# Two-layer recurrence-and-attention trunk on one core: the first probability scalings are pinned behind the second half of q on ScalarE, and their transposes move one chunk on

## The chip, the core and the metric

The kernel runs on one core of one Trainium2 chip. Five engines work side by side on it: TensorE (PE in the rows; its weight loads are PEld), VectorE (DVE), ScalarE (ACT), GpSimd (POOL) and SyncE (SP, which here only starts DMAs). Each engine takes its own instructions strictly in their order and waits on semaphores for the others. The metric is the device time of one execution in microseconds (us).

## The reference

A token batch of 256 x 1024 in float32 runs through two equal layers. Cut to what matters here:

```
for each of 2 layers:
    h  = rms_norm(x)                     # 256 x 1024
    z  = h @ w_in                        # one combined input projection
    A) recurrent half (width 512):
       x = causal_depthwise_conv(z_x, conv_w) + conv_b          # 4 taps
       r, i = sigmoid(x @ w_r), sigmoid(x @ w_i)                # block-diagonal
       h_t = a_t * h_(t-1) + sqrt(1 - a_t^2) * (i * x)_t        # a = exp(-8 r softplus(-lam))
       out_A = h * silu(z_g)
    B) attention half (width 512, 8 query heads of 64, 2 kv heads):
       q, k with rms_norm and partial rotary positions
       compressed branch: blocks of 32 tokens -> two small products -> kc, vc; softmax over blocks
       selected branch:   gathered key blocks, softmax;  window branch: softmax
       out_B = (g0 * o_cmp + g1 * o_sel + g2 * o_win) * silu(z_n)
    x = x + concat(out_A, out_B) @ w_out
```

With 256 tokens, the selected blocks and the window cover all keys that a token may see, and the kernel computes both branches with dense causal attention: softmax probabilities of the scores, each multiplied by its gate over its row sum.

## The kernel before

**Products.** Each large projection is done as three products (`mm3`, L175 to L177) of a high and a low part of both operands. For each 128-column piece of the weights, a "chunk", SP loads it to `raw`, the high part `wh` is a ScalarE cast (L167) or a second DMA by POOL, and VectorE computes the low part `wl` (L170, "the split"). Chunk by chunk, TensorE multiplies 8 pieces of the input by these, 24 products of 128x256 each.

**Chunks.** In each layer some chunks for keys, values, queries and the compressed branch come first. Then come twelve chunks of the recurrent input and of the two gate paths, in the order x0, x1, x2, x3, n0, n1, g0, g1, g2, g3, n2, n3 (numbers 0 to 11), then eight of the output projection (12 to 15 for its first half). The work around a chunk is planned in `plan[n]`, with two lists: one traced ahead of chunk n, one in its middle. The numbers in the table `SL` say where a piece stands: for instance `turn` holds for each of the eight attention pairs (i, t) the chunk ahead of which its probabilities are transposed, i being one of four pairs of query heads and t one of two halves of the tokens; each (i, t) has four score matrices, two heads in two branches. A scheduler then decides the order on each engine from the order of tracing and from dependencies, so a piece can end up a little before or behind its planned place.

**Pieces that the change or the rows touch.**

- `qk_transpose(t)` (t = 0 planned at chunk 0, t = 1 at chunk 2): TensorE transposes keys and queries into PSUM buffers `pp` (there are two). Per kv head ScalarE casts the keys (`kd`, L375 and L376) and VectorE computes their low part (`kl`, L377). Likewise per kv head ("half") the queries, on ScalarE (`qs`, L384) and VectorE (`qs` low part, L385). L387 copies `qT`.
- `att_scores(i, t)`: three products into PSUM (L581, L582, L583), row maxima on VectorE (L586, L588), exponentials on ScalarE into `pr` (L594).
- `att_coef(i, t)`: VectorE makes gate over row sum (L599, L600), ScalarE scales the probabilities by it (L607, four instructions).
- `att_turn(i, t)`: TensorE transposes the scaled probabilities into a `pp` buffer (L620), ScalarE copies them to `pt` (L83).
- The compressed branch: `cmp_act` (L470 `hth` on ScalarE, L472 `hs` on VectorE), `cmp_kv` (L477, L478 products of `hs`, then small steps on VectorE, POOL and ScalarE up to the copy `kcd`, L495), `cmp_kt` (L499, the transpose of `kcd`, and L501), its scores (L511 to L533) and their transposed probabilities `pct`.
- `rg_x(j)`: VectorE writes `xpad` (L652), ScalarE starts the convolution `cx` (L653), VectorE adds three taps (L655). `rg_gates(j)`: L663, two products per j of `cx`, planned at chunks 2 to 5, then activations (L666 on).
- Splits of chunks x2, x3 and n0, n1 are ordered behind `L.qk_done`, the last subtraction of `qk_transpose`.

Of the kernel before, what the change touches and what calls it, by code (L numbers as in the profile page):

```python
# [14 lines left out]
AF = mybir.ActivationFunctionType  # L15
# [9 lines left out]
HD = 64  # L25
# [13 lines left out]
for _n, _w in (("g", 8), ("cw", 16), ("cb", 4), ("br", 4), ("bi", 4), ("lam", 4)):  # L39
# [11 lines left out]

K = dict(scale="A", ev1="A", hid="A", pct="A")
SL = dict(qk=(0, 2), order=("x0", "x1", "x2", "x3", "n0", "n1", "g0", "g1", "g2", "g3", "n2", "n3"),
          cmp=(2, 3, 4), att=(1, 3, 3, 4, 6, 7, 10, 11), turn=(2, 4, 5, 6, 8, 10,
          12, 13), cs=(5, 5), cpt=6, aout=(7, 15), gates=(2, 3, 4, 5), tab=6, sqrt=5,
          scan=8, rout=(9, 11))

# [14 lines left out]
def hybrid_trunk_kernel(ctx: ExitStack, tc: tile.TileContext, vx, wc, wt, wv, wf, wo, w1, w2, pe,  # L72
# [6 lines left out]
    V, A, G, T = nc.vector, nc.scalar, nc.gpsimd, nc.tensor  # L79
# [10 lines left out]
    def bank(tag, bufs, shape=(P, 512), dt=F32):  # L90
        return ps.tile(list(shape), dt, name=tag, tag=tag, bufs=bufs)
# [166 lines left out]
    def layer(l, prev):  # L258

        L = Layer()  # L260
# [105 lines left out]
        def qk_transpose(t):  # L366
            zn = L.zn[t]
            tok = slice(t * P, (t + 1) * P)
            pk = bank("pp", 2)
            for i in range(2):  # L370
                T.transpose(pk[:, i * P:(i + 1) * P],
                            zn[:, 8 + 2 * i:10 + 2 * i].rearrange("p h d -> p (h d)"), ident)
            for g in range(2):
                src = pk[g * HD:(g + 1) * HD, :2 * P].rearrange("p (b s) -> p b s", s=P)
                A.copy(L.kd[:HD, g, :, tok], src)  # L375
                A.copy(L.kd[HD:, g, :, tok], src)  # L376
                V.tensor_tensor(kl[:HD, g, :, tok], src, L.kd[:HD, g, :, tok].bitcast(F32), op=ALU.subtract)  # L377
            pq = bank("pp", 2)
            for i in range(4):
                T.transpose(pq[:, i * P:(i + 1) * P], zn[:, 2 * i:2 * i + 2].rearrange("p h d -> p (h d)"),  # L380
                            ident)
            for g in range(2):
                src = pq[g * HD:(g + 1) * HD].rearrange("p (i s) -> p i s", s=P)
                A.copy(L.qs[:HD, g::2, tok], src)  # L384
                L.qk_done[t] = V.tensor_tensor(L.qs[HD:, g::2, tok], src, L.qs[:HD, g::2, tok].bitcast(F32),  # L385
                                               op=ALU.subtract)
            A.copy(L.qT[:, :, tok], pq.rearrange("p (i s) -> p i s", s=P))  # L387
# [209 lines left out]
        def att_coef(i, t):  # L597
            pr, sm = L.att[i, t]
            V.reciprocal(sm[:, 2], sm[:, 1])  # L599
            V.tensor_tensor(sm[:, 3].rearrange("p (g b) -> p g b", g=2), L.gate[:, t, i, :, 1:3],  # L600
                            sm[:, 2].rearrange("p (g b) -> p g b", g=2), op=ALU.mult)
            for g in range(2):
                for b in range(2):
                    sc_ = sm[:, 3, 2 * g + b:2 * g + b + 1]
                    e = K["scale"][(2 * g + b) % len(K["scale"])]
                    if e == "A":
                        A.activation(pr[g][:, b], pr[g][:, b], AF.Copy, scale=sc_)  # L607
                    else:
                        V.tensor_scalar(pr[g][:, b], pr[g][:, b], sc_, None, op0=ALU.mult)

# [142 lines left out]
        for k in range(KT):  # L753
            b = []
# [22 lines left out]
        def at(n, f, *a, mid=False):  # L777
            plan[n][1 if mid else 0].append(F(f, *a))

        at(1, cmp_hid)  # L780
        at(SL["qk"][0], qk_transpose, 0)
        at(SL["qk"][1], qk_transpose, 1)
        for n, f in zip(SL["cmp"], (cmp_act, cmp_kv, cmp_kt)):
            at(n, f)
        for q in range(8):
            i, t = divmod(q, 2)
            n = SL["att"][q]
            at(n, att_scores, i, t)
            at(n, att_coef, i, t, mid=True)
        at(SL["cs"][0], cmp_scores)  # L790
        at(SL["cpt"], cmp_pt)
        for q in range(8):
# [24 lines left out]
    for l in range(DEPTH):  # L817
        prev, st_ = layer(l, prev)
        prev0 = prev0 or prev
        steps += st_  # L820
# [140 lines left out]
```

## Time and profile before

| | |
|---|---|
| time, median of 3 runs | 250.75 us (250.7 to 250.95) |
| the profiled execution's own time | 250.6 us |
| its span, from first to last instruction | 248.8 us |
| granted TensorE clock, mean of the span | 0.998 |
| TensorE busy | 241.5 us, 97% of the span |
| VectorE, ScalarE, POOL busy | 195.7, 163.9, 40.6 us |

The profile shows one execution. Its span begins with the first instruction of an engine and ends with the last; the device time holds 1.8 us more. A row of a timeline gives the start of an instruction in us from the start of the span, its duration, the engine, the line, the operation, the tile written and the tile read, shapes, a count where neighbours with one form stand together, and in brackets the time that the engine had stood idle before it and what released it. Ends of matmuls are modelled.

### The profile page before, as it was taken

The page shows a single profiled execution, that of the slowest core. Times are in us where ns is not written, and L with a number is a line of the kernel's source. Part 1 is how long each engine was busy: PE and PEld are TensorE (multiplying, and loading weights), DVE is VectorE, ACT ScalarE, POOL GpSimd, SP SyncE. Part 2 cuts the span into 40 slices and gives each one's busy share as a digit, 9 for nine tenths or more (in the row PEclk, how much of TensorE's full clock was granted, in tenths as well). Part 3 has the DMA queues.
Part 4 walks back from the last instruction along what each step waited for, and adds up shares of the span by engine and source line. Part 5 has one row for each costly group of instructions (what it writes and reads, how often), then busy time and mean ns, then how long its engine had stood idle before and what let it go on. Part 6 is the DMA issues. An engine that isn't in the chain of part 4 may idle for free.

```text
span 248.8 us, 5206 instructions
## 1 busy us (share of the span) xinstructions
PE 241.5 (97%) x1958; PEld 222.2 (89%) x1958; DVE 195.7 (79%) x379; ACT 163.9 (66%) x414; POOL 40.6 (16%) x65
## 2 busy tenths in 40 slices
PE   8999999989999999999999999998999999999994
PEld 3999998967998899989999999996889989998993
DVE  5998897789999997555995569688998998875322
ACT  6957429799999968623863553849999996860000
POOL 0027540001901011000001054100100001010000
PEclk9999999999999999999999999999999999999999
DMA  6988999846599778841569968575259848960022
GB/s 216 365 300 261 362 414 402 256 151 192 200 302 401 263 230 277 258 131 52 169 211 354 309 227 263 166 228 188 99 167 335 323 124 262 339 205 19 3 84 84
DMA packets 17593, 57.17 MB, mean 230 GB/s; under 512 B 2208, under 2 KB 3360, under 8 KB 17056
## 3 DMA queue, kind: packets, MB, share of 16 engines
q1 hardware_dynamic: 12816, 39.86, 46.9%
q0 software_dynamic: 4608, 16.78, 21.2%
q8 instruction: 15, 0.25, 0.4%
q10 hardware_dynamic: 144, 0.20, 0.2%
q14 instruction: 10, 0.08, 0.1%
HBM read 55.78 MB, written 1.05 MB: 228 GB/s over the span
## 4 chain that ended last, share of the span: by engine, by line
PE 66%; ACT 14%; DVE 9%; DMA 4%; POOL 3%; issue 2%; SPq 0%; ACTq 0%; DVEq 0%; POOLq 0%
PE fm L175 12%; PE fm L176 12%; PE fm L177 11%; PE pp L620 4%; PE s L175 3%; PE s L177 3%; PE s L176 3%; PE m L634 3%; DVE wl L170 3%; ACT pr L594 3%; DMA ga<-in_gains_dram 2%; ACT qs L384 2%; PE m L637 1%; PE m L640 1%; PE pp L177 1%
## 5 line engine op out<-in xcount | busy, mean ns | idle before, releaser
L170 DVE TENSOR_TENSOR wl<-raw,wh 128x1024 fp32r<-128x1024 f32 (+4 forms) x67 | 74.5, 1118 | 7.4 <-ACT wh L167 3.0
L175 PE MATMUL fm<-hh,wh 128*128 128x256 f32 x192 | 56.9, 296 | 0.1
L176 PE MATMUL fm<-hl,wh 128*128 128x256 f32 x192 | 55.1, 287 | 0.0
L177 PE MATMUL fm<-hh,wl 128*128 128x256 f32 x192 | 54.4, 284 | 0.0
L167 ACT CAST wh<-raw 128x768 fp32r<-128x768 f32 (+4 forms) x34 | 30.5, 896 | 25.4 <-DMA raw<-in_wc_dram 7.0
L175 PEld LDWEIGHTS fm<-hh,wh 128*128 128x128 f32 x192 | 36.7, 191 | 1.4 <-issue 0.8
L176 PEld LDWEIGHTS fm<-hl,wh 128*128 128x128 f32 x192 | 36.8, 191 | 0.5 <-issue 0.4
L177 PEld LDWEIGHTS fm<-hh,wl 128*128 128x128 f32 x192 | 36.7, 191 | 0.0
L594 ACT ACTIVATE pr<-s,sm 128x128 f32<-128x128 f32 (+1 forms) x64 | 25.9, 417 | 7.7 <-DVE sm L588 5.4
L175 PE MATMUL fm<-yy,wh 128*128 128x256 f32 x96 | 27.4, 285 | 0.0
L176 PE MATMUL fm<-yy,wh 128*128 128x256 f32 x96 | 27.0, 281 | 0.0
L177 PE MATMUL fm<-yy,wl 128*128 128x256 f32 x96 | 26.9, 280 | 0.0
L607 ACT ACTIVATE pr<-pr,sm 128x128 f32<-128x128 f32 (+1 forms) x64 | 23.7, 455 | 2.1 <-DVE sm L600 2.0
L175 PEld LDWEIGHTS fm<-yy,wh 128*128 128x128 f32 x96 | 18.1, 188 | 0.8 <-issue 0.8
L156 POOL DMA_DIRECT2D wh<-in_wo_dram x16 | 8.4, 528 | 61.2 <-PE fm L177 26.5
L176 PEld LDWEIGHTS fm<-yy,wh 128*128 128x128 f32 x96 | 18.1, 188 | 0.0
L177 PEld LDWEIGHTS fm<-yy,wl 128*128 128x128 f32 x96 | 18.1, 188 | 0.0
L176 PE MATMUL s<-wl,hh 128*128 128x384 f32 x48 | 16.7, 348 | 0.3 <-DVE wl L170 0.3
L156 POOL DMA_DIRECT2D wh<-in_wf_dram x16 | 9.0, 563 | 47.0 <-PE fm L177 23.4
L177 PE MATMUL s<-wh,hl 128*128 128x384 f32 x48 | 16.1, 336 | 0.0
L620 PE MATMUL pp<-cst,pr 128*128 128x128 f32 x96 | 15.0, 276 | 1.2 <-DVE kl L377 1.2
L729 DVE TENSOR_TENSOR head<-head,fm 128x512 f32<-128x512 f32 x11 | 7.6, 687 | 10.7 <-PE fm L177 10.7
(206 smaller groups left out, 614.9 us busy)
## 6 DMA issues: line engine op xcount, KB each, us to landing
raw<-in_wf_dram SPq DMA_DIRECT2D x24, 512.0 KB, 4.4
wh<-in_wf_dram POOLq DMA_DIRECT2D x16, 512.0 KB, 4.5
raw<-in_wo_dram SPq DMA_DIRECT2D x16, 512.0 KB, 4.8
wh<-in_wo_dram POOLq DMA_DIRECT2D x16, 512.0 KB, 4.8
raw<-in_wt_dram SPq DMA_DIRECT2D x15, 384.0 KB, 4.2
yy<-in_w_dram SPq DMA_DIRECT2D x4, 1024.0 KB, 7.1
raw<-in_wc_dram SPq DMA_DIRECT2D x4, 512.0 KB, 5.3
raw<-in_wv_dram SPq DMA_DIRECT2D x4, 420.0 KB, 4.6
```

Of the source, the lines that this page charges most:

```text
L156: G.dma_start(self.wh, self.src)
L167: A.copy(hi[:, c], self.raw[:, c])
L170: V.tensor_tensor(lo[:, c], self.raw[:, c], hi[:, c].bitcast(F32), op=ALU.subtract)
L175: T.matmul(o, lh, rh, start=start, stop=False)
L176: T.matmul(o, lh, rl, start=False, stop=False)
L177: T.matmul(o, ll, rh, start=False, stop=stop)
L384: A.copy(L.qs[:HD, g::2, tok], src)
L594: A.activation(pr[g][:, b], ov[:, b], AF.Exp, bias=sm[:, 0, 2 * g + b:2 * g + b + 1], accum_out=sm[:, 1, 2 * g + b:2 * g + b + 1])
L607: A.activation(pr[g][:, b], pr[g][:, b], AF.Copy, scale=sc_)
L620: T.transpose(pp[:, (2 * g + b) * P:(2 * g + b + 1) * P], pr[g][:, b, c * P:(c + 1) * P], ident)
L634: T.matmul(o[g * HD:(g + 1) * HD], L.vv[:, 0, b, g * HD:(g + 1) * HD], pt[:, g, b, 0:2].rearrange("p a s -> p (a s)"), start=h == b == 0, ...
L729: V.tensor_tensor(x_sb[:, m], x_sb[:, m], os_[0].rearrange("p (a s) -> p a s", a=2), op=ALU.add)
```

## The change

The last cast of a q half on ScalarE is remembered as `L.qs_done`. The coefficients and scalings of the first pair (0, 0) are no longer planned in the middle of chunk 1 (x1) but ahead of chunk 2 (x2), after `qk_transpose(1)`, and the four scalings are ordered behind the second half of q: no semaphore, only a place in ScalarE's queue. The transposes of that pair are planned at chunk 3 instead of 2. This holds in both layers.

```
-          cmp=(2, 3, 4), att=(1, 3, 3, 4, 6, 7, 10, 11), turn=(2, 4, 5, 6, 8, 10,
+          cmp=(2, 3, 4), att=(1, 3, 3, 4, 6, 7, 10, 11), turn=(3, 4, 5, 6, 8, 10,
           12, 13), cs=(5, 5), cpt=6, aout=(7, 15), gates=(2, 3, 4, 5), tab=6, sqrt=5,
...
             for g in range(2):
                 src = pq[g * HD:(g + 1) * HD].rearrange("p (i s) -> p i s", s=P)
-                A.copy(L.qs[:HD, g::2, tok], src)
+                L.qs_done = A.copy(L.qs[:HD, g::2, tok], src)
...
                     if e == "A":
-                        A.activation(pr[g][:, b], pr[g][:, b], AF.Copy, scale=sc_)
+
+                        with tc.issue_after(L.qs_done.ins) if i == t == 0 else nullcontext():
+                            A.activation(pr[g][:, b], pr[g][:, b], AF.Copy, scale=sc_)
...
             at(n, att_scores, i, t)
-            at(n, att_coef, i, t, mid=True)
+            if q == 0:
+                at(SL["qk"][1], att_coef, i, t)
+            else:
+                at(n, att_coef, i, t, mid=True)
```

Lines behind the pinned scalings have numbers higher by 2 after the change (L607 is L609, L620 is L622, L653 is L655, L663 is L665).

The order of instructions shows what the scheduler makes of it. ScalarE, layer 0, around chunks x1 and x2 before the change (`kd` and `qs` are key and query casts of token half 1, `pr` the probabilities of pair (0, 0), `cx` the convolution):

```order
L376 CAST kd_122<-pp 64x2x128
L607 ACTIVATE pr<-pr,sm 128x128 x4
L653 ACTIVATE cx<-xpad_72,head 128x256
L375 CAST kd_122<-pp 64x2x128
L376 CAST kd_122<-pp 64x2x128
L384 CAST qs<-pp 64x4x128
L470 ACTIVATE hth<-m 128x160
L666 ACTIVATE rr<-fm,hb 128x256
L667 ACTIVATE tmp_747<-fm,hb 128x256
L669 ACTIVATE tl<-rr,sp 128x256
L83 COPY pt<-pp 128x4x128
L384 CAST qs<-pp 64x4x128
```

The same place after the change:

```order
L376 CAST kd_122<-pp 64x2x128
L655 ACTIVATE cx<-xpad_72,head 128x256
L384 CAST qs<-pp 64x4x128
L375 CAST kd_122<-pp 64x2x128
L376 CAST kd_122<-pp 64x2x128
L470 ACTIVATE hth<-m 128x160
L668 ACTIVATE rr<-fm,hb 128x256
L384 CAST qs<-pp 64x4x128
L609 ACTIVATE pr<-pr,sm 128x128 x4
L387 COPY qT<-pp 128x4x128
L669 ACTIVATE tmp_740<-fm,hb 128x256
```

The four scalings moved from ahead of the second key half to behind the second q half, and that q half moved from behind three gate activations and the `pt` copy to behind one gate activation.

TensorE, layer 0, at the end of chunk x2 before the change (`fm` products are those of the chunk, `s` are scores, `m` the compressed branch):

```order
L177 MATMUL fm<-hh,wl 128x256
L620 MATMUL pp<-cst,pr 128x128 x4
L175 MATMUL fm<-hh,wh 128x256
L176 MATMUL fm<-hl,wh 128x256
L177 MATMUL fm<-hh,wl 128x256
L175 MATMUL fm<-hh,wh 128x256
L176 MATMUL fm<-hl,wh 128x256
L177 MATMUL fm<-hh,wl 128x256
L581 MATMUL s<-kd_122,qs 128x512
L477 MATMUL m<-w2s,hs 32x64
L478 MATMUL m<-w2s,hs 128x64
L582 MATMUL s<-kl,qs 128x512
```

After the change the scores that follow the whole of chunk x2 end like this, and chunk x3 begins:

```order
L581 MATMUL s<-kd_122,qs 128x256
L582 MATMUL s<-kl,qs 128x256
L583 LDWEIGHTS identb
L583 MATMUL s<-maskb,identb 128x256
L622 MATMUL pp<-cst,pr 128x128 x4
L665 MATMUL fm<-cx,rws 128x256 x2
L175 MATMUL fm<-hh,wh 128x256
```

The transposes of pair (0, 0) moved from the middle of x2's products to behind the scores, and the scores of pair (1, 0), of 256 columns, moved up from behind x3 to stand here.

VectorE, layer 1, around the weight splits of the first gate chunks, before:

```order
L600 TENSOR_TENSOR sm<-gate,sm 128x4
L501 TENSOR_TENSOR kcb<-m,cst 128x32
L655 SCALAR_TENSOR_TENSOR cx<-xpad_72,head,cx 128x256
L586 TENSOR_REDUCE sm<-s 128x2
L655 SCALAR_TENSOR_TENSOR cx<-xpad_72,head,cx 128x256
L586 TENSOR_REDUCE sm<-s 128x2
L170 TENSOR_TENSOR wl<-raw,wh 128x1024 x2
L599 RECIPROCAL sm<-sm 128x4
```

And after:

```order
L600 TENSOR_TENSOR sm<-gate,sm 128x4
L501 TENSOR_TENSOR kcb<-m,cst 128x32
L586 TENSOR_REDUCE sm<-s 128x2 x2
L170 TENSOR_TENSOR wl<-raw,wh 128x1024
L657 SCALAR_TENSOR_TENSOR cx<-xpad_72,head,cx 128x256
L170 TENSOR_TENSOR wl<-raw,wh 128x1024
L657 SCALAR_TENSOR_TENSOR cx<-xpad_72,head,cx 128x256
L599 RECIPROCAL sm<-sm 128x4
L170 TENSOR_TENSOR wl<-raw,wh 128x1024
L657 SCALAR_TENSOR_TENSOR cx<-xpad_72,head,cx 128x256
```

The three taps of the last `cx` of the layer moved behind and between weight splits; their consumers are the gate products planned at chunk 5.

## Rows read from the trace of the kernel before

**Rows 1.** The page: busy time, share of the span and number of instructions of each engine; the granted clock in 40 slices (tenths); the shares by engine of the chain that ended last.

```profile
PE 241.5 (97%) x1958; PEld 222.2 (89%) x1958; DVE 195.7 (79%) x379; ACT 163.9 (66%) x414; POOL 40.6 (16%) x65
...
PEclk9999999999999999999999999999999999999999
...
PE 66%; ACT 14%; DVE 9%; DMA 4%; POOL 3%; issue 2%; SPq 0%; ACTq 0%; DVEq 0%; POOLq 0%
```

**Rows 2.** Timeline of TensorE, layer 0, end of chunk x2 and start of x3 (at 56.05). Columns: start us, duration us, engine, line, operation, written and read tiles, partitions of weights and products, shape, count, idle time before.

```profile
50.23 0.28 PE L176 MATMUL fm<-hl,wh 128*128 128x256 f32 x1
50.35 0.28 PE L177 MATMUL fm<-hh,wl 128*128 128x256 f32 x1
51.54 0.63 PE L620 MATMUL pp<-cst,pr 128*128 128x128 f32 x4 [0.91 <-DVE kl L377]
...
53.03 0.30 PE L477 MATMUL m<-w2s,hs 128*32 128x64 f32 x2
53.26 0.43 PE L478 MATMUL m<-w2s,hs 128*128 128x64 f32 x2
...
53.95 1.03 PE L663 MATMUL fm<-cx,rws 128*128 128x256 f32 x4
54.63 0.58 PE L581 MATMUL s<-kd,qs 128*128 128x512 f32 x1
...
56.05 0.36 PE L175 MATMUL fm<-hh,wh 128*128 128x256 f32 x1
```

**Rows 3.** Timeline of ScalarE, layer 0, same place: scalings, `cx`, key and query casts, a gate activation.

```profile
48.12 1.28 ACT L607 ACTIVATE pr<-pr,sm 128x128 f32<-128x128 f32 x4
49.31 0.59 ACT L653 ACTIVATE cx<-xpad,head 128x256 f32<-128x256 f32 x1
49.92 0.37 ACT L375 CAST kd<-pp 64x256 fp32r<-64x256 f32 x1
...
50.69 0.58 ACT L384 CAST qs<-pp 64x512 fp32r<-64x512 f32 x1
...
51.37 0.46 ACT L666 ACTIVATE rr<-fm,hb 128x256 f32<-128x256 f32 x1
...
53.17 0.58 ACT L384 CAST qs<-pp 64x512 fp32r<-64x512 f32 x1
```

**Rows 4.** Timeline of VectorE, layer 0: `hs` and the last q subtraction.

```profile
52.53 0.32 DVE L472 SCALAR_TENSOR_TENSOR hs<-hth,m 128x160 f32<-128x160 f32 x1
...
53.79 0.69 DVE L385 TENSOR_TENSOR qs<-pp,qs 64x512 fp32r<-64x512 f32 x1 [0.45 <-ACT qs L384]
```

**Rows 5.** Timeline of TensorE, layer 0, end of chunk x3.

```profile
59.01 0.40 PE L581 MATMUL s<-kd,qs 128*128 128x512 f32 x1
...
59.60 1.03 PE L663 MATMUL fm<-cx,rws 128*128 128x256 f32 x4
60.56 0.24 PE L499 MATMUL m<-cst,kcd 32*128 32x32 f32 x1
...
61.30 0.28 PE L583 MATMUL s<-maskb,identb 128*128 128x256 bf16 x1
61.87 0.39 PE L581 MATMUL s<-kd,qs 128*128 128x256 f32 x1 [0.28 <-ACT pr L594]
```

**Rows 6.** Timeline of TensorE, layer 1: end of x2, then end of x3 (n0 starts at 181.03).

```profile
170.41 0.28 PE L177 MATMUL fm<-hh,wl 128*128 128x256 f32 x1
171.50 0.30 PE L477 MATMUL m<-w2s,hs 128*32 128x64 f32 x2 [0.80 <-DVE hs L472]
...
172.04 0.63 PE L620 MATMUL pp<-cst,pr 128*128 128x128 f32 x4 [0.25 <-DVE kl L377]
...
179.57 0.60 PE L663 MATMUL fm<-cx,rws 128*128 128x256 f32 x2
180.10 0.24 PE L499 MATMUL m<-cst,kcd 32*128 32x32 f32 x1
...
181.03 0.39 PE L175 MATMUL fm<-hh,wh 128*128 128x256 f32 x1
```

**Rows 7.** Timeline of VectorE: the copy of `kcd` in layer 0 and in layer 1.

```profile
59.98 0.20 DVE L495 COPY kcd<-kcd 32x64 f32<-32x64 f32 x1
...
179.62 0.18 DVE L495 COPY kcd<-kcd 32x64 f32<-32x64 f32 x1
```

**Rows 8.** Timeline of VectorE, layer 1: `hs`.

```profile
171.12 0.32 DVE L472 SCALAR_TENSOR_TENSOR hs<-hth,m 128x160 f32<-128x160 f32 x1
```

**Rows 9.** Timeline of ScalarE, layer 1: eight scalings, of pairs (0, 1) and (1, 0).

```profile
181.62 2.88 ACT L607 ACTIVATE pr<-pr,sm 128x256 f32<-128x256 f32 x8
```

**Rows 10.** What leads to the gate products of chunk 5. Timelines of VectorE and TensorE, layer 1, then layer 0: the last taps of `cx`, a row maximum, two weight splits, the gate products.

```profile
184.12 0.69 DVE L586 TENSOR_REDUCE sm<-s 128x2 f32<-128x512 f32 x1
184.72 2.35 DVE L170 TENSOR_TENSOR wl<-raw,wh 128x1024 fp32r<-128x1024 f32 x2
...
188.31 1.02 PE L663 MATMUL fm<-cx,rws 128*128 128x256 f32 x4
...
69.20 0.47 DVE L655 SCALAR_TENSOR_TENSOR cx<-xpad,head,cx 128x256 f32<-128x256 f32 x1
...
69.88 1.03 PE L663 MATMUL fm<-cx,rws 128*128 128x256 f32 x4
```

**Rows 11.** Timeline of VectorE, layer 1: a weight split that waited for its transfer.

```profile
190.56 1.23 DVE L170 TENSOR_TENSOR wl<-raw,wh 128x1024 fp32r<-128x1024 f32 x1 [0.54 <-DMA raw<-in_wf_dram]
```

## The prediction, made before the changed kernel ran

> **What bounds the kernel now.** I read the page first, then the chain of work that ended last, then the timelines of TensorE, ScalarE and VectorE around the first attention scores of each layer. On the page the reader is to see that TensorE is busy 97% of the span at the full granted clock (2.4 GHz), that it carries 66% of the chain, and that ScalarE and VectorE together carry 23% of it [rows 1]. So time can only be won where TensorE stands still because one of those two is late. Its timeline is read by starts: within a chunk one 128x256 product starts 0.12 us after the other [rows 2], so a longer distance is a hole. Four holes lie where the change works, two in each layer.
>
> Layer 0, end of chunk x2: the product at 50.35 is followed by the transposes of the first probabilities only at 51.54, so 1.07 us are lost [rows 2]. They wait for a PSUM buffer `pp` that the second key half (kl) still has to leave; kl is late because the four scalings (48.12 to 49.31) stand ahead of the second half's casts on ScalarE [rows 3]. Layer 0, end of x3: a score product of (2,0) waits from 61.42 to 61.87, 0.45 us [rows 5]. Layer 1, end of x2: hs, the compressed-key input, holds L477 from 170.53 to 171.50, 0.97 us, and the transposes follow 0.54 us later where 0.23 us is usual (53.03 to 53.26), 0.31 us more [rows 2, 6].
>
> How long a hole is depends on the reading. The idle column gives 0.91, 0.28, 0.80 and 0.25 us, 2.24 together [rows 2, 5, 6]; starts give 1.07, 0.45, 0.97 and 0.31, 2.80. I take starts, since the idle column counts from a modelled end of a product, 0.28 us after its start, while the next may begin after 0.12. The Trainium skill, "Perfetto Trace Analysis", section "Tensor Engine Instruction (MATMUL, LD_WEIGHTS)", says the same of that end: it is estimated from the size, not observed. By the idle column at most 2.24 us are to be won, by starts 2.80.
>
> **The change, part by part.** No instruction is added or removed; the scalings of (0,0) and their transposes move in both layers, and the scheduler moves others round them.
>
> *Layer 0, end of x2.* On ScalarE cx and the first q cast take the place of the scalings. Step by step, with the distances of [rows 3]: cx starts at 48.0 to 48.1, where the scalings did; q's first half 48.65; kd twice 49.15 and 49.53; hth 49.9; rr 50.1; q's second half 50.6, where it started at 53.17 before; then the scalings, 51.1 to 52.3. On VectorE the second q subtraction can follow that cast (0.58 long) at 51.2, and hs stands right behind it: 51.9 to 52.24, where it began at 52.53 [rows 4]. TensorE no longer has transposes there. It finishes the six products of x2 that are left (the order above has them behind the transposes) at 50.47 + 6 x 0.12 = 51.19, does the first score product (512 columns, at least 0.24) and is ready for L477 at 51.5, but hs lets it go at 52.3. So the hole does not close; it moves to hs and measures 0.8 us: gain 1.07 - 0.8, about 0.27. The gate products at 53.95, four of 256 columns, took 0.68 us to the next start where four times 0.12 would do [rows 2]; the new order takes them and the scores apart, which I put at 0.13 of these 0.20. Chunk x3 starts at 55.65 instead of 56.05: **0.40**. The transposes themselves (0.38) lie after the scores now, near 54.5, 2 us after the last scaling: that wait is gone for good.
>
> *Layer 0, end of x3.* The product of (2,0) is no longer placed there (0.45 saved), and the gate pair takes 0.68 instead of the 0.96 us from 59.60 to 60.56 [rows 2, 5]: 0.73 together. But L499 comes first now and needs kcd. From the start of hs to the end of the copy of kcd VectorE took 60.18 - 52.53 = 7.65 us [rows 4, 7]; without the q subtraction and its wait between (0.69 + 0.45) it ends near 58.5, and TensorE arrives at 55.65 + 2.96 = 58.61. The edge is so close that I allow 0.16: **0.57**.
>
> *Layer 1, end of x2.* By the same steps hs ends at 171.27 instead of 171.44 [rows 8]: kl no longer waits for a kd that stood behind the scalings, but q's first subtraction, two more cx and the second kl precede hs. L477 starts at 171.33, a hole of 0.80 for 0.97; and the 0.31 before the transposes goes: **0.48**.
>
> *Layer 1, end of x3.* The gate pair of 179.57 to 181.03 is torn apart by L499 and costs 1.46 us with it [rows 6]; in one piece, with L499 at 0.2 beside it, it is 0.88: 0.6 saved. The copy of kcd ended at 179.80 [rows 7] and comes 0.6 to 0.9 earlier, near 179.0, TensorE needs it at 178.7: 0.3 given back. **0.30**.
>
> *What is late next.* Chunk n0 of layer 1 starts near 180.2, and after six products the transposes of (0,1) ask for scalings that start at 180.85 (0.77 before 181.62: cx, 0.6 long, moved behind them, the rest from the earlier queue [rows 9]); the first of eight is done 0.36 later, at 181.21, and TensorE asks at 180.2 + 0.72: 0.3 lost. Then the gates of chunk 5: their input is the third cx. Before, ScalarE wrote cx ahead of the eight scalings, and VectorE had left the third cx by 184.12, long before L663 at 188.31 [rows 10]. Now cx follows the scalings (180.85, plus 2.88 less 0.09 that neighbours overlap, plus 0.6, gives 184.25), and two weight splits, 2.35 us together, stand between the VectorE steps of 0.42 (0.47 less an overlap [rows 10]): 184.25 + 3 x 0.42 + 2.35 = 187.85. TensorE is there 7.28 us after n0 and those 0.3, at 187.75: 0.1 lost. Layer 0 had only 69.67 to 69.88 of slack at that place [rows 10] and gets one split more ahead of the last cx, but its queue starts about as much earlier; I allow 0.15. **-0.55.** The copy of the compressed probabilities, behind which att_out starts in layer 1, gets a pt copy ahead of the table load; I take it like a q cast, 0.58 for 512 elements too [rows 3]; five products (0.6 us) moved ahead of att_out cover it. If they did not, it would cost about 0.5.
>
> *Sum:* 0.40 + 0.57 + 0.48 + 0.30 - 0.55 = 1.20 us. The profiled execution took 250.6 us (its span 248.8, 1.8 around it), the median of the three runs is 250.75, 0.15 above it. So 250.75 - 1.20 = 249.55, and I say **249.5 us**. No DMA is moved past another on SP's or POOL's queue; the raw and wh buffers are loaded chunks ahead, and only one split in these stretches waited for its transfer (0.54 us at 190.56 [rows 11]).
>
> **The rivals.** First, *the wait only changes its name*: hs holds TensorE as long as the transposes did, kcd takes the 0.73 and the 0.6 of the x3 ends, the gates of chunk 5 the rest. For it: three of the four places are met by less than 0.3 us. Against it: the hole before the transposes cannot come back, and hs stands 0.6 us earlier in layer 0 by rows whose distances are known. It leaves about 0.4 us: 250.35. The Trainium skill, "Perfetto Trace Analysis", section "Identifying the Most-Contended Engine", advises to work on the most contended engine first; by that rule a change which takes nothing off TensorE would bring nothing, and the holes above are what speaks against it here.
>
> Second, *more is won*: kcd, the scalings of (0,1) and the gates arrive in time, since ScalarE and VectorE too run ahead. Then 1.20 + 0.16 + 0.3 + 0.55 = 2.2 us are won: 248.55. For it: in layer 0 the ScalarE queue gains up to 1 us. Against it: in layer 1 it gains less.
>
> Third, *slower*: the third cx of chunk 5. Each split ahead of it that waits for its raw transfer, as the one at 190.56 did, adds 0.54 us, and each split put ahead adds 1.17, half of the pair. Both layers have one more ahead now; if both count in full and one transfer is late, 2.35 + 0.54 - 0.3 makes some +2.6 against -1.75: 251.5. It decides for slower from 2.25 us of lateness together (1.75 won elsewhere, 0.5 to be measurable). Against it: the raw buffers free earlier by the same shift.
>
> That the change does not do what it says is excluded by the order: the scalings stand behind the second q cast in both layers.
>
> **How the numbers follow.** Forecast 249.5 (248.9 to 250.1): 0.45. Changed name, 250.35: 0.24, half of it under the bound. More won, 248.55: 0.17. Slower, 251.5: 0.10. The remaining 0.04 is no case I can name, around no change. A measurement of this kernel can tell about 0.2%, 0.5 us, from no change: faster is below 250.25, slower above 251.25. Faster: 0.43 + 0.12 + 0.17 = 0.72. Same: 0.02 + 0.12 + 0.04 = 0.18. Slower: 0.10. The range runs from the second rival's time less 0.15 for its unknowns to a first rival with one split counted (249.5 + 1.17): 248.4 to 250.65.
>
> **What would show it.** In the changed profile: L620's transposes (now L622) of (0,0) with no idle time ahead of them; hs at about 51.9 and 170.95 and L477 as the product that waits, some 0.8 us in both layers; x3 at 55.65 and 174.85, n0 near 60.9 and 180.2; a small wait at L499. Wrong would be: L477 later than 52.6, a wait of over 0.5 us at L499, or one at the gate products of chunk 5 (now L665) near 68.7 or 187.7.

## The result and the profile after

The changed kernel took **249.57 us** (median of 4 runs, 249.29 to 249.84), the kernel before beside it 250.72 us. By the medians it is 1.15 us faster. The ratio, with its 95% interval in brackets, is 0.9938 (0.9918 to 0.9957); here and below it is an estimate of its own and differs a little from the quotient of the two medians, which is 0.9954. The forecast was 249.5 us, faster. In a second comparison (e9 below) the two took 249.76 and 250.98 us, 1.22 us, a ratio of 0.9948 (0.9928 to 0.9969).

The page after, busy time by engine and the chain by engine, answers to [rows 1]:

```profile
PE 240.9 (97%) x1958; PEld 222.3 (90%) x1958; DVE 196.1 (79%) x379; ACT 163.9 (66%) x414; POOL 39.2 (16%) x65
...
PE 76%; ACT 9%; DVE 9%; DMA 2%; issue 2%; SPq 1%; DVEq 0%; ACTq 0%
```

By the counts no engine has fewer instructions to do. TensorE's share of the chain grew from 66% to 76%, and ScalarE's fell from 14% to 9%. What TensorE waited for says more. The view of waits of TensorE, before (us in total, times, longest), and after:

```profile
PE pp L620 <- DVE kl L377: 1.2, 2, 0.9
...
PE m L477 <- DVE hs L472: 0.8, 1, 0.8
PE s L581 <- ACT pr L594: 0.3, 1, 0.3
```

```profile
PE m L477 <- DVE hs L472: 1.7, 2, 0.8
```

The waits for the key half (`kl`) and for the exponentials are gone, and hs, which held TensorE in one layer, now holds it in both.

**Where the time went.** Two traces can't be compared at one time of their clocks, because the part ahead of layer 0 isn't equally long in each: the changed one comes to the first product of the compressed branch 0.26 us later. So I measure between five products that stand at the same place in both orders: the first of `cmp_act` in layer 0, the last score product of 256 columns in layer 0, the second score product of layer 1, `cmp_act` of layer 1 and the last score product of 256 columns there. Timeline of TensorE, before:

```profile
47.18 0.44 PE L468 MATMUL m<-cst,hid 128*128 128x160 f32 x2
...
89.82 0.37 PE L581 MATMUL s<-kd,qs 128*128 128x256 f32 x1
...
162.55 0.37 PE L581 MATMUL s<-kd,qs 128*128 128x256 f32 x1
...
166.52 0.44 PE L468 MATMUL m<-cst,hid 128*128 128x160 f32 x2
...
209.25 0.37 PE L581 MATMUL s<-kd,qs 128*128 128x256 f32 x1
```

The same products after:

```profile
47.44 0.44 PE L468 MATMUL m<-cst,hid 128*128 128x160 f32 x2
...
89.40 0.36 PE L581 MATMUL s<-kd,qs 128*128 128x256 f32 x1
...
161.75 0.36 PE L581 MATMUL s<-kd,qs 128*128 128x256 f32 x1
...
165.72 0.44 PE L468 MATMUL m<-cst,hid 128*128 128x160 f32 x2
...
208.24 0.36 PE L581 MATMUL s<-kd,qs 128*128 128x256 f32 x1
```

Three stretches come out of it: attention of layer 0 (first to second row), what lies between the layers' attention ("between", second to third), and attention of layer 1 (fourth to fifth). They took 42.64, 72.73 and 42.73 us before, and 41.96, 72.35 and 42.52 after: **0.68, 0.38 and 0.21 us won**, 1.27 together, of which the later start of 0.26 takes its part back. The table has the same three for every kernel that ran. The kernels marked * are executions in which TensorE waited 0.55 us for a weight split at 38.6 to 38.9 us. Two kernels ran both ways: the first stretch is 0.38 us shorter in e9 than in the same changed kernel above, and 0.28 in e7 than in e10. TensorE comes late to the hole at hs there and finds less of it: its idle time is 0.46 us in e9 and 0.84 above. So the marked ones are compared among themselves, and the kernel before has no marked execution.

| kernel | layer 0 | between | layer 1 |
|---|---|---|---|
| before | 42.64 | 72.73 | 42.73 |
| changed | 41.96 | 72.35 | 42.52 |
| changed, again (e9) * | 41.58 | 72.36 | 42.50 |
| only the transposes moved (e1) | 43.18 | 72.72 | 42.75 |
| only the scalings moved (e2) * | 42.37 | 72.36 | 43.06 |
| change in layer 0 alone (e3) | 41.97 | 72.36 | 42.67 |
| change in layer 1 alone (e4) * | 42.24 | 72.74 | 42.53 |
| before, transposes of (3,1) joined (e5) | 42.68 | 73.31 | 42.66 |
| changed, without the pin (e6) * | 41.60 | 72.35 | 42.56 |
| changed, hs between the q halves (e7) * | 41.59 | 72.36 | 42.53 |
| the same again (e10) | 41.87 | 72.35 | 42.50 |
| and hs earlier in layer 1 (e8) | 41.86 | 72.35 | 42.44 |
| and kcd earlier (e11) | 42.85 | 72.36 | 42.51 |
| and later transposes of (0,1), (1,0) (e12) | 43.83 | 72.36 | 42.95 |

**Layer 0, end of x2 and x3.** TensorE after, which answers to [rows 2, 5]:

```profile
51.45 0.40 PE L581 MATMUL s<-kd,qs 128*128 128x512 f32 x1
52.68 0.30 PE L477 MATMUL m<-w2s,hs 128*32 128x64 f32 x2 [0.84 <-DVE hs L472]
...
54.92 0.60 PE L622 MATMUL pp<-cst,pr 128*128 128x128 f32 x4
55.35 1.03 PE L665 MATMUL fm<-cx,rws 128*128 128x256 f32 x4
56.03 0.47 PE L175 MATMUL fm<-hh,wh 128*128 128x256 f32 x1
...
59.18 0.24 PE L499 MATMUL m<-cst,kcd 32*128 32x32 f32 x1
...
61.32 0.47 PE L175 MATMUL fm<-hh,wh 128*128 128x256 f32 x1
```

ScalarE and VectorE there, which answer to [rows 3, 4]:

```profile
50.91 0.58 ACT L384 CAST qs<-pp 64x512 fp32r<-64x512 f32 x1
51.39 1.28 ACT L609 ACTIVATE pr<-pr,sm 128x128 f32<-128x128 f32 x4
```

```profile
51.58 0.69 DVE L385 TENSOR_TENSOR qs<-pp,qs 64x512 fp32r<-64x512 f32 x1
52.30 0.32 DVE L472 SCALAR_TENSOR_TENSOR hs<-hth,m 128x160 f32<-128x160 f32 x1
```

The second q cast starts at 50.91 where it started at 53.17, the scalings stand behind it, and hs stands behind the last q subtraction. TensorE is through with the first score product at 51.69 (51.45, and 0.24 to the next start where no hole is) and waits to 52.68, 0.99 us by starts. The transposes of (0,0) run at 54.92 without a wait.

**Layer 1.** TensorE after, which answers to [rows 6]:

```profile
170.71 0.30 PE L477 MATMUL m<-w2s,hs 128*32 128x64 f32 x2 [0.82 <-DVE hs L472]
...
174.30 0.47 PE L175 MATMUL fm<-hh,wh 128*128 128x256 f32 x1
...
178.39 0.24 PE L499 MATMUL m<-cst,kcd 32*128 32x32 f32 x1
...
179.70 0.47 PE L175 MATMUL fm<-hh,wh 128*128 128x256 f32 x1
```

### The profile page after: what moved, and what is told of

Same layout as the page of the kernel before. It is cut to its first block, busy times and chain, and to the rows that moved or that the text cites. A ratio compares the mean times of both kernels' runs of the same rounds, so it can differ in the third digit from the quotient of the medians.

```text
span 247.8 us, 5200 instructions
## 1 busy us (share of the span) xinstructions
PE 240.9 (97%) x1958; PEld 222.3 (90%) x1958; DVE 196.1 (79%) x379; ACT 163.9 (66%) x414; POOL 39.2 (16%) x65
## 3 DMA queue, kind: packets, MB, share of 16 engines
HBM read 55.78 MB, written 1.05 MB: 229 GB/s over the span
## 4 chain that ended last, share of the span: by engine, by line
PE 76%; ACT 9%; DVE 9%; DMA 2%; issue 2%; SPq 1%; DVEq 0%; ACTq 0%
PE fm L175 13%; PE fm L176 13%; PE fm L177 13%; PE pp L622 4%; PE s L176 4%; PE s L177 4%; PE s L175 4%; PE m L636 3%; DVE wl L170 2%; DMA raw<-in_wt_dram 2%; PE s L582 2%; PE fm L665 2%; PE s L581 2%; PE pp L177 2%; DVE cx L657 2%
## 5 line engine op out<-in xcount | busy, mean ns | idle before, releaser
L609 ACT ACTIVATE pr<-pr,sm 128x128 f32<-128x128 f32 (+1 forms) x64 | 23.8, 452 | 2.3 <-DVE sm L600 2.3
L175 PE MATMUL s<-wh,hh 128*128 128x384 f32 x48 | 15.4, 344 | 0.1
```

The source lines that it names most:

```text
L175: T.matmul(o, lh, rh, start=start, stop=False)
```

## The experiments

After the result the theories were these. **A**: the gain is the sum of TensorE's holes, each set by the queues of ScalarE and VectorE; the change takes some and hs is the next. Its rivals: **B**, one of the two moves alone brings it (B with the transposes, B' with ScalarE's order); **C**, the terms of the forecast hold as they stand, and what happens at 101 us has its cause in an earlier ScalarE or VectorE; **D**, each wait only changes its name; **E**, the pin brings it; **G**, a later copy to pt costs more than it gives.

### One move without the other (e1, e2)

```
 e1, against the kernel before:
-  turn=(2, 4, 5, 6, 8, 10,
+  turn=(3, 4, 5, 6, 8, 10,
 e2, against the changed kernel:
-  turn=(3, 4, 5, 6, 8, 10,
+  turn=(2, 4, 5, 6, 8, 10,
```

> Only the transposes of pair (0,0) are planned one chunk later; the scalings stay where they were before. Theory A (the gain is the sum of TensorE's holes, each set by ScalarE's and VectorE's queue): the second key half and the second q half still stand behind the scalings on ScalarE, hs still starts near 52.5 in layer 0, so the wait goes from the transposes to hs almost whole; gain 0.3 to 0.6 us, 250.3. Theory B (the later transposes alone bring it, the pin is an accessory): the whole gain, 249.5 to 249.7.

> The scalings are planned at x2 and pinned behind q, but their transposes stay at chunk 2. Theory A: TensorE now waits for the scalings inside x2: in layer 0 a hole of 1.1 us from 50.4 and 0.2 more at each further transpose, L477 not before 52.9; in layer 1 some 1.6 us; what the x3 ends win (0.5 and 0.2) and the unbroken transposes at 101 (0.36) pay for most of it: 250.45, within 0.5. Theory B' (ScalarE's order is all): 249.5.

Measured, with the kernel before at 250.92 us: e1 251.27 us, ratio 1.0011 (0.9997 to 1.0025); e2 250.98 us, ratio 1.0000 (0.9987 to 1.0014). Neither half brings anything that can be measured, so B and B' fall. Both numbers miss theory A's too, e1 by 1 us, e2 by 0.5. TensorE of e1, layer 0, end of x2, and the gate products of chunk 5:

```profile
52.02 0.52 PE L620 MATMUL pp<-cst,pr 128*128 128x128 f32 x3 [0.19 <-DVE kl L377]
...
53.04 0.50 PE L581 MATMUL s<-kd,qs 128*128 128x512 f32 x1 [0.50 <-DVE qs L385]
...
53.70 0.30 PE L477 MATMUL m<-w2s,hs 128*32 128x64 f32 x2
...
70.80 1.13 PE L663 MATMUL fm<-cx,rws 128*128 128x256 f32 x4
```

With the scalings still ahead, the same lateness holds TensorE further on: first kl again (0.19 us idle), then the q subtraction (0.50). That a hole moves with the late queue is theory A; that it stops at these two, and not at hs, it had not foreseen. Nor had it counted the place at 70.80, where the gate products start 0.45 us behind the product ahead of them; a little earlier (69.42 to 69.62) a product behind transposes takes 0.20. The late cx of chunk 5, which ends at 70.74, costs about 0.25 there: it is the place of the forecast's third rival. The first stretch is 0.54 longer than before; no run takes the rest apart. TensorE of e2 at the transposes of (0,0), layer 0 and layer 1:

```profile
51.66 0.33 PE L622 MATMUL pp<-cst,pr 128*128 128x128 f32 x1 [0.71 <-ACT pr L609]
...
171.79 0.33 PE L622 MATMUL pp<-cst,pr 128*128 128x128 f32 x1 [1.66 <-ACT pr L609]
```

The first waits for the scalings as expected. In layer 1 this costs 0.33 us against the kernel before (43.06 for 42.73) and 0.56 against the changed one, in layer 0 0.13 (42.37 against 42.24 in e4, which has the order of before there), and the stretch between gives 0.38 back.

### One layer alone (e3, e4)

```
 against the changed kernel; N is 0 in e3, 1 in e4
-  with tc.issue_after(L.qs_done.ins) if i == t == 0 else nullcontext():
+  with tc.issue_after(L.qs_done.ins) if i == t == 0 and l == N else nullcontext():
...
-  if q == 0:
+  if q == 0 and l == N:
...
-  at(SL["turn"][q], att_turn, *divmod(q, 2))
+  at(2 if q == 0 and l == 1 - N else SL["turn"][q], att_turn, *divmod(q, 2))
```

> The change in layer 0 alone, layer 1 as before. Theory A, by the comparison of the two traces at equal TensorE work: 0.18 at the end of x2, 0.54 at the end of x3, nothing lost after it up to 78 us, and 0.36 at 101 us where the transposes of pair (3,1) stand in one piece instead of four: 1.05 us, 249.7. Theory C (the recorded terms of layer 0 as they stand: 0.40 + 0.57 - 0.15): 0.82 us, 249.9, and no difference at 101 us.

> The change in layer 1 alone, layer 0 as before. Theory A: 0.22 us, 250.5, and layer 0 with the transposes at 101 us in four pieces as before. Theory C (the recorded terms of layer 1: 0.48 + 0.30 - 0.40): 0.38 us, 250.35.

Measured, beside 250.92: e3 249.74 us, ratio 0.9950 (0.9935 to 0.9965), 1.18 us; e4 250.70 us, ratio 0.9987 (0.9974 to 1.0000), 0.22 us. By the table e3 wins 0.67 and 0.37 in the first two stretches, e4 0.2 in the third and nothing in the second; its first has no marked partner with the order of before. The interval of e4 reaches 1, so its 0.2 us rests on the trace. Both numbers are nearer to theory A (1.05 and 0.22) than to C (0.82 and 0.38), and C's "no difference at 101 us" is wrong. So five sixths of the gain comes from the change in layer 0, and over a third of that lies 50 us behind the change.

### What lies at 101 us (e5)

Here ScalarE and TensorE of the kernel before, then of the changed one: the scalings of pair (3,1) and its eight transposes, at the start of chunk 12. The third row is TensorE's weight load, which shows its wait:

```profile
100.94 1.71 ACT L607 ACTIVATE pr<-pr,sm 128x256 f32<-128x256 f32 x4 [0.70 <-DVE sm L600]
...
101.50 0.44 PE L620 MATMUL pp<-cst,pr 128*128 128x128 f32 x2
...
101.50 0.20 PEld L620 LDWEIGHTS pp<-cst,pr 128*128 128x128 f32 x2 [0.22 <-ACT pr L607]
```

```profile
98.09 1.71 ACT L609 ACTIVATE pr<-pr,sm 128x256 f32<-128x256 f32 x4 [0.50 <-DVE sm L600]
...
100.89 1.03 PE L622 MATMUL pp<-cst,pr 128*128 128x128 f32 x8
```

Before, the transposes stood in four pairs between single products. My theory was that each change between the two costs TensorE 0.1 us. The experiment joined them in the kernel before:

```
-  T.transpose(pp[...],
+  L.last_turn = T.transpose(pp[...],
...
-  products(e, ks)
+  with tc.issue_after(L.last_turn.ins) if l == e == half == 0 and n == 1 else nullcontext():
+      products(e, ks)
```

> The kernel before, with one thing else: in layer 0 the products of chunk 13 are ordered behind the last transpose of pair (3,1), so that these eight transposes stand in two pieces (2 and 6) instead of four pieces between single products. ScalarE and VectorE keep their order. Theory A (each change between transposes and products costs TensorE about 0.1 us, and the 0.36 us at 101 us comes from there): 0.25 to 0.35 us faster than the kernel before. Theory C (the 0.36 at 101 us has another cause, an earlier ScalarE or VectorE): no difference, within 0.1.

Measured: 251.68 us beside 250.86, ratio 1.0025 (1.0010 to 1.0041): slower, and the stretch between the layers 0.58 longer. TensorE's weight loads of e5 there:

```profile
102.28 0.20 PEld L620 LDWEIGHTS pp<-cst,pr 128*128 128x128 f32 x2 [0.22 <-ACT pr L607]
...
103.22 0.64 PEld L620 LDWEIGHTS pp<-cst,pr 128*128 128x128 f32 x6 [0.39 <-ACT pr L607]
```

That theory falls, and C's "within 0.1" with it. The pairs stood apart because their scalings came apart, and joined they wait for the later ones. By the rows, what wins the 0.37 is that the scalings start 2.85 us earlier (98.09 against 100.94; 0.42 of it is the lead that TensorE has there anyway, 89.40 against 89.82), the earlier ScalarE that C had named: with the change in layer 0 the scheduler puts the scalings of (3,0) ahead of all four exponentials of (3,1) and the gate of (3,1) ahead of the next weight split on VectorE. It does so in e2, e3 and e6, which plan the first scalings at x2, and not in e1. In the table every kernel that plans them so in layer 0 has 72.35 or 72.36 there, and every other 72.72 or more. No run moved the scalings at 98 us alone, so this cause is read from the rows and not shown by itself, and why the scheduler's choices 50 us on depend on the plan at x2 was not tried.

### The pin (e6)

```
-  with tc.issue_after(L.qs_done.ins) if i == t == 0 else nullcontext():
+  with nullcontext():
```

> The changed kernel without the pin: the scalings are planned at x2, the transposes at chunk 3, but the scheduler is free. It puts one of four scalings (layer 1: two) ahead of the second q cast. Theory A: that cast and hs come 0.3 us later, and what is lost is no more than that per layer: 249.6 to 250.1, 0.7 to 1.2 us faster than the kernel before. Theory E (the pin is what brings the time): at most 0.3 us faster than the kernel before.

Measured: 249.71 us beside 250.86, ratio 0.9956 (0.9938 to 0.9973), 1.15 us faster, with 41.60 and 42.56 in the two attention stretches, against 41.58 and 42.50 of the changed kernel. E falls: the pin gives at most 0.1 us. Planning the scalings at x2 and the transposes at chunk 3 does it, since the scheduler then puts three of the four scalings (in layer 1 two) behind the second q cast by itself.

### The next wait: hs, kcd (e7 to e10)

```
 e7, e10, against the changed kernel, in qk_transpose (e8: g == 1 - l)
   for g in range(2):
+      if t == 1 and g == 1:
+          cmp_act()
       src = pq[g * HD:(g + 1) * HD].rearrange("p (i s) -> p i s", s=P)
...
-  for n, f in zip(SL["cmp"], (cmp_act, cmp_kv, cmp_kt)):
+  for n, f in zip(SL["cmp"][1:], (cmp_kv, cmp_kt)):
```

> The changed kernel with the tanh and hs of the compressed branch traced between the two q halves: in layer 0 hs now stands ahead of the last q subtraction on VectorE, the products of hs ahead of the first score product; nothing else moves but a qT copy. Theory A (hs alone holds TensorE in layer 0 after the change): hs from 51.58 instead of 52.30, L477 at 51.97 instead of 52.68, and with the score product of 0.24 behind it 0.45 us are won: 249.1, and L477 of layer 1 still waits 0.8. Theory D (the wait only changes its name): the second score product now waits for the last q subtraction, 0.1 or nothing is won: 249.5.

> As the kernel with hs between the q halves, and in layer 1 hs traced ahead of both, so that it stands ahead of the first q half's last cx and the second kl on VectorE. Theory A: in layer 1 L477 starts 0.8 us earlier without a wait; two groups of transposes are split more often (0.2 to 0.3 lost): 0.5 us more than the kernel with hs between the halves in layer 0 alone, 248.6. Theory D: the q subtractions, 0.35 us later, become the wait: nothing more is won, 249.1.

> The changed kernel once more, beside the three that follow. Theory A: again 1.0 to 1.4 us faster than the kernel before, and from the row of the first scores in layer 0 (42.5 us before) to the end the trace is 1.2 to 1.3 us shorter, wherever that row itself starts.

> The kernel with hs between the two q halves again, now beside the changed kernel. Theory A: 0.3 to 0.4 us faster than the changed kernel (0.37 by equal TensorE work in the earlier trace: hs no longer holds TensorE in layer 0, the copy of kcd takes 0.3 to 0.5 of the 0.85 back). Theory D (it is the same time): within 0.15 us of the changed kernel.

Measured: e7 249.51 us (ratio 0.9952, 0.9935 to 0.9969) and e8 249.65 (0.9942, 0.9922 to 0.9962) beside 250.86; e9, the changed kernel, 249.76 (0.9948, 0.9928 to 0.9969), as expected, and e10 249.54 (0.9942, 0.9922 to 0.9963) beside 250.98. The difference of e10 to the changed kernel, 0.2 us, is inside both intervals. The trace of e9 was not as expected: from the first score product of layer 0 on it is 1.97 us shorter than before instead of 1.2 to 1.3, as a marked execution that makes up in layer 0 what it lost ahead of it. The table tells more: in layer 0 e7 stands at 41.59 against 41.58 and e10 at 41.87 against 41.96. TensorE of e7, layer 0 (lines here are two higher):

```profile
51.81 0.30 PE L479 MATMUL m<-w2s,hs 128*32 128x64 f32 x2
...
55.40 0.47 PE L175 MATMUL fm<-hh,wh 128*128 128x256 f32 x1
...
58.93 0.22 PE L501 MATMUL m<-cst,kcd 32*128 32x32 f32 x1 [0.31 <-DVE kcd L497]
```

The mechanism of A is right, its sum isn't. The hs products start at 51.81 with no wait in this marked execution; in e10, the same kernel unmarked, TensorE still stands idle for 0.35 us there. Counted from the first product of `cmp_act`, x3 starts 0.5 us earlier than in the changed kernel (7.73 us after it where e9 has 8.22; 8.11 in e10 where the unmarked changed kernel has 8.59). At the end of x3 the copy of kcd holds TensorE 0.31 us, n0 starts only 0.14 earlier in both, and at the end of the stretch 0 to 0.09 us are left: D, by way of kcd. In layer 1, too, e8 exchanges one wait for another. TensorE of e8, the second score product and the first transpose of (0,0):

```profile
171.38 0.47 PE L583 MATMUL s<-kd,qs 128*128 128x512 f32 x1 [0.57 <-DVE qs L387]
...
172.65 0.33 PE L624 MATMUL pp<-cst,pr 128*128 128x128 f32 x1 [0.44 <-ACT pr L611]
```

hs is early, and the q subtraction that it overtook and the scalings are late: 42.44 against 42.50, 0.06 us won.

### kcd earlier, and the transposes of (0,1) later (e11, e12)

```
 e11, against e10, in cmp_kv: the step that writes vcb moves behind the copy of kcd
-  V.tensor_tensor(L.vcb, pkc[:, None, HD:2 * HD].to_broadcast([P, 8, HD]), ...
...
   V.tensor_copy(kd[:, 1], kd[:, 0])
+  V.tensor_tensor(L.vcb, pkc[:, None, HD:2 * HD].to_broadcast([P, 8, HD]), ...
 e12, against e11:
-  turn=(3, 4, 5, 6, 8, 10,
+  turn=(3, 5, 6, 6, 8, 10,
```

> As the one before, and on VectorE the 0.67 us step that writes vcb stands behind the steps that lead to kcd instead of ahead of them. Theory A (kcd is what holds TensorE at the end of x3 once hs is gone): the wait of L499's transpose (0.31 in layer 0) goes, 0.4 us more in layer 0, in layer 1 up to 0.2: 0.7 to 0.9 us faster than the changed kernel. Theory D (scores of (1,0), behind it, wait instead): 0.1 or nothing more than hs between the halves.

> As the one before, and the transposes of pairs (0,1) and (1,0) one chunk later each (chunks 5 and 6 instead of 4 and 5). Theory A (TensorE waits for the scalings of (0,1) in layer 1, the recorded term of 0.3): these eight transposes then run in one piece without a wait, 0.3 us less in layer 1, none in layer 0: 1.0 to 1.2 us faster than the changed kernel. Theory G (the copies to pt and the output products come late instead): no faster than the kernel before it, or up to 0.5 slower.

Measured: e11 250.93 us, ratio 0.9994 (0.9980 to 1.0009); e12 252.06 us, ratio 1.0037 (1.0022 to 1.0052). The whole gain of the change is gone in e11, and more in e12: neither theory had that. kcd did come in time in e11 (TensorE no longer waits for it, and its product L501 starts at 58.47 where e10 has 58.94). But the scalings of (0,1) start hardly earlier, at 60.99 for 61.09, and the transposes that need them come 0.97 us behind the last gate product instead of 0.69: 0.28 of that lead is lost again, theory D once more. The larger loss comes right behind, in this order: VectorE, POOL (three rows), ScalarE, TensorE (two rows) of e11:

```profile
62.00 1.44 DVE L602 TENSOR_TENSOR sm<-gate,sm 128x4 f32<-128x4 f32 x1
...
62.12 0.74 POOL L247 TENSOR_TENSOR sg<-ga,cst 128x96 f32<-128x96 f32 x2
62.82 0.60 POOL L249 TENSOR_TENSOR ga<-ga 128x192 f32<-128x192 f32 x1
63.38 0.28 POOL L250 TENSOR_TENSOR ga<-ga 32x48 f32<-32x48 f32 x1
...
63.54 1.28 ACT L611 ACTIVATE pr<-pr,sm 128x128 f32<-128x128 f32 x4 [0.84 <-DVE sm L602]
...
67.65 0.66 PE L624 MATMUL pp<-cst,pr 128*128 128x128 f32 x4 [0.47 <-ACT pt L83]
...
70.49 1.13 PE L667 MATMUL fm<-cx,rws 128*128 128x256 f32 x4 [0.18 <-DVE cx L659]
```

VectorE's product of gate and row sum, 4 columns, took 1.44 us. In e10 it took 0.35, and one of POOL's instructions was long instead (VectorE, POOL):

```profile
61.85 0.35 DVE L602 TENSOR_TENSOR sm<-gate,sm 128x4 f32<-128x4 f32 x1
...
63.40 1.28 POOL L250 TENSOR_TENSOR ga<-ga 32x48 f32<-32x48 f32 x1
```

The median of L602 over the 16 of a run is 0.155. Meanwhile POOL made tables for the next layer. In e11 and e12 the scheduler has also put the first two of these table products (L247) ahead of the issue of a weight DMA that stands ahead of all four in e10. The scalings of (1,0) then start at 63.54, cx behind them is late, and TensorE waits before the transposes at 67.65 and at the gates of chunk 5, at 70.49. e12 shows the same 1.45 us on VectorE. The Trainium skill, "SBUF — State Buffer", section "SBUF: two separate sides", says that a VectorE operation with two SBUF inputs and a GpSimd operation that reads SBUF exclude one another for a whole instruction; the trace agrees in that L602 ends at 63.44 and L249 at 63.42, but no run here tested it by itself. POOL's L250 fits: 1.28 us in e10, where VectorE does weight splits from 63.33 on, and 0.28 in e11, where it takes row maxima from PSUM. The stretch in layer 0 is 0.98 longer than in e10, the median 1.39; the profiled execution, 250.38 us, is one of the fastest of its 12, so the trace accounts for about 1 us. That the long L602 makes this loss is a reading of the chain, not shown by a run, and e12's further 1 us was not taken apart; the longest wait of TensorE in its layer 0 is 0.82 us at 69.22, for a ScalarE copy (L516). No version beat the changed kernel by more than can be measured.

## Why the prediction was right, and where its steps were not

- **The total.** Forecast 1.20 us, measured 1.15 and 1.22. The table's three stretches make 1.27. But the forecast had 0.82 in layer 0, nothing between and 0.38 in layer 1, and the runs show 0.68, 0.38 and 0.21. Without the 0.38 between the layers, which the forecast doesn't contain, its local steps would have given 0.9 us and a time near 249.85, still inside the range. That the sum agrees to 0.1 is in part luck.
- **End of x2: mis-sized, in both layers.** x3 of layer 0 starts at 56.03, and less the 0.26 of the later start at 55.77 where 55.65 was forecast: 0.28 won for 0.40. In layer 1 it starts 1.03 earlier, of which 0.80 had been won ahead of it: 0.23 for 0.48. The step that was mis-sized is the hole that stays at hs: 0.99 and 0.98 us by starts, not 0.80. In layer 0 hs came 0.14 later than worked out (52.30 less 0.26 against 51.9), in layer 1 it came no earlier at all (4.61 us behind the first product of `cmp_act`, 4.60 before). The 0.13 for gates and scores that stand apart was not won at the gates, which take 0.68 us to the next start as before (55.35 to 56.03). The mechanism, the hole that moves from the transposes to hs, is in the rows above.
- **End of x3: right, in layer 0 only together with what follows.** Layer 0: 0.68 for the whole stretch less 0.28 leaves 0.40 for all that lies behind x2, forecast 0.57 - 0.15 = 0.42. Layer 1: n0 starts 1.33 earlier, 0.30 more than x3, as forecast. By starts L499 is met by a hole of 0.2 us in layer 1, where 0.3 was forecast, and of 0.1 in layer 0.
- **What is late next: about right in layer 1.** From n0 on (1.33) to the last score product (1.01) 0.32 us are lost, forecast 0.40. At the first compressed scores (L511, 185.06 before and 184.00 after) the lead is 1.06, so 0.27 of it is lost in n0, where the transposes of (0,1) wait for their scalings; the gates of chunk 5, at 187.50, have no hole. In layer 0 nothing singles out the 0.15 that was allowed there.
- **The copy of pct and att_out** cost nothing, as said.
- **"The scheduler moves others round them" was followed too short a way.** The order on ScalarE and TensorE at 98 to 101 us could be read before the run, and so could the wait of the transposes there for their scalings. The prediction followed it only near the change and at the gates of chunk 5. This is the step that failed: a term of +0.38, absent from the sum.
- **The rivals.** "More is won" didn't happen: of its three terms only the gates came in time, while the scalings of (0,1) and, in layer 1, kcd were late about as foreseen, and the hole at hs was longer. "The wait only changes its name" is false for the change as a whole and true for the next step, e7 and e8. "Slower" by the third cx of chunk 5 didn't happen here but does in e1 and e11, at 70.80 and 70.49, so the place was well named. The reading beside the first rival, that a change which takes nothing off TensorE brings nothing, did not hold: TensorE has the same 1958 products, and the time went out of its holes.

## What to carry over

Where one engine is busy 97% of the time, read its holes by start times and then the queue of the engine that is late: a few instructions moved back in that queue won 0.5%, while removing the next hole (hs) only showed the one behind it (kcd). If a scheduler makes the order, compare the order over the whole program, not only round the change: a third of this gain lay 50 us further on, and a small edit in e11, meant to win time, cost all of it. Two moves that bring nothing alone (e1, e2) can bring the whole gain together.

## What the runs showed of the hardware that I had not expected

- The way to the same product in layer 0 differed by 0.8 us between executions with the same order up to there: 47.18 to 47.98 us in the 14 profiled ones. In the five with a wait of 0.55 us for a weight split at 38.6 to 38.9 us, 0.3 to 0.4 of it was made up in the holes of layer 0. A single profile's span therefore can't tell 0.4 us. The distance between two fixed products can, among executions that lost the same ahead of them (42.64 and 42.68, 41.96 and 41.97 for the same order), but not across the two groups (41.96 and 41.58).
- A VectorE instruction on 128x4 elements took 1.44 us, nine times its median, while POOL multiplied tables; in e10 it was a POOL instruction of 32x48 elements that took 1.28 us for 0.28, beside a weight split on VectorE.
